# DeltaNet merges in freed buffers, block-wise residual squares, earlier parameters

## The chip, the cores and the metric

The kernel runs on one core of a Trainium2 chip, in one launch. The metric is device time in microseconds (us), from the start of an execution to its end. The engines are TensorE (PE, matmul, with its weight loads as PEld), VectorE (DVE), ScalarE (ACT), GpSimd (POOL) and SyncE (SP, which only issues DMAs here). Each engine runs its own instructions in a fixed order and waits on the others by semaphores. Data sit in SBUF (128 partitions) and in eight PSUM banks, which TensorE writes.

## The reference

A two-layer block for 512 tokens of width 1024: 256 context tokens and 256 latent tokens. Only the latent tokens are returned, so layer 1 needs its context tokens up to the token mixers only. Per layer:

```
mod  = split(silu(c) @ mod_w + mod_b, 6)             # one row for latents, one for context
p    = (rms_norm(h, norm1_g) * (1 + mod[1]) + mod[0]) @ in_w     # (512, 1024) x (1024, 11 K)
y_b  = retention(p), rg_lru(p), gated_deltanet(p), rwkv7(p)       # four branches of width 512
m    = sum_b sigmoid(p_gates_b + gate_b) * (y_b @ branch_w[b])
h    = h + mod[2] * (m @ out_w)
u    = rms_norm(h, norm2_g) * (1 + mod[4]) + mod[3]
h    = h + mod[5] * ((silu(u @ w1) * (u @ w3)) @ w2)
```

The result is `rms_norm(h_latent, final_norm_g)`. The DeltaNet branch has four heads; each works in chunks of tokens, with an inverse of a triangular matrix per chunk and a state that passes from chunk to chunk, in both directions.

## The kernel before

All activations lie transposed: features on partitions, tokens on the free axis. A dense product takes a block of 128 x 128 weights against 512 columns (layer 0) or 256 (layer 1, where only latents are needed). For precision each operand is split into a high and a low part, and a block needs three matmuls: wh·XH, wh·XL and wl·XH (`dense`). Weights are packed on the host in the order of use, in units of 8 blocks (512 KB). `raw` loads a unit on SyncE's queue, `unit` makes wh by a ScalarE cast (L400) and wl by a VectorE subtract (L361). Units are taken in turn from the pools in `wps`: the first one, wp, always, and a second where `more_weights` has opened one.

The work is a list of tasks that `_phases` writes out by hand: `first`, `seq1` (RWKV, retention and RG-LRU with gates ahead), `seq2` (DeltaNet heads `gd` and merges `mg`), `seqo` (output projection `ow`), `seqf` (ffn). `ga(b,d)` computes a gate of branch b ahead of its merge and stores it to HBM (gd), from where `merge` loads it again (t<-gd); `mg(b,d)` does the products of a branch's output with branch_w for two feature blocks, multiplies by the gates and adds into M. `merge_open` loads a branch's output (yt, from HBM's yd) and splits it into YH and YL. A planner then orders the instructions of all engines: among those ready it takes what stands first in the program, so a later task can fill an engine while an earlier one waits. Weight and modulation loads (`early`) go ahead of other work. On the chip each engine keeps that order.

In `layer`, `seq2` runs inside the DeltaNet pool gp with PSUM pools pc2 (two banks, chains) and pd2 (a third dense accumulator `d`). A head `gd` is a serial chain: small matmuls of the inverse into one PSUM tile `mg`, then a loop over four chunks with `Z`, `R` and the state `St` (PSUM tile `ch`), then `headnorm` with transposes (L1260) and `put_y` (L301), which stores the head's output (yd<-to). After seq2 gp is closed, and on its bytes open hh (the residual H, loaded at L1541, and temporaries t2), wo (a second weight pool), mqo (modulation weights) and op (MH, ML, the split of M). A tile of a new pool on old bytes waits for the users of the closed pools there. By the sizes in the code, base pools take about 68 KB of a partition, mp (M, YH, YL, yt, t2) 46 in layer 0 and 27 in layer 1, and gp 92 and 102.

`mod` computes one of the six modulation vectors: weights of 512 KB per k as `mraw` (L592), 4 matmuls per k into the one bank `mg`, a transpose (L603). In layer 0 they stand between other tasks. `squares` squares the eight blocks of H on ScalarE (tile t) and adds them on VectorE; `rms_bcast` sums over partitions by matmuls into `st`, takes the inverse root on VectorE (`sm`), and spreads it by more `st` matmuls; `norm` writes XH and XL. `setup` prepares constants; `load_params` loads a layer's small parameters P, `params_mu` and `params` derive more from them.

Of the kernel before, what the change touches and what calls it, by code (L numbers as in the profile page):

```python
# [11 lines left out]
F32R = mybir.dt.float32r  # L12
# [6 lines left out]
DEPTH = 2  # L19
# [95 lines left out]
def _phases(l):  # L115

    last = l + 1 == DEPTH
    first = _mod(0, 1, 1, 0) + _mod(0, 4, 2) if l == 0 else []
    if last:
        seq1 = [("rws",), ("kvr", 0), ("kvr", 1), ("rw", 0), ("rt", 0), ("lr", 0), *_ga(3, 0, 2), ("kvr", 2), ("rw", 1), ("rt", 1), ("lr", 1), *_ga(3, 2, 4), ("kvr", 3), ("rw", 2), ("rt", 2), ("lr", 2), *_ga(3, 4, 6), ("rw", 3), ("rt", 3), ("lr", 3), *_ga(3, 6, 8)]  # L120
    else:
        seq1 = [("rws",), ("kvr", 0), ("kvr", 1), ("rw", 0), ("rt", 0), ("lr", 0), *_ga(3, 0, 2), ("kvr", 2), ("rw", 1), ("rt", 1), ("lr", 1), *_ga(3, 2, 4), *_ga(0, 0, 2), ("kvr", 3), ("rw", 2), ("rt", 2), ("lr", 2), *_ga(3, 4, 6), *_ga(0, 2, 4), ("rw", 3), ("rt", 3), ("lr", 3), *_ga(3, 6, 8), *_ga(0, 4, 8), *_ga(2, 0, 4)]
    if last:
        seq2 = [*_mg(0, 0, 4), ("gab",), ("gd", 0), ("gd", 1), *_mg(0, 4, 8), *_mg(3, 0, 4), ("gd", 2), *_mg(3, 4, 8), ("gd", 3), *_ga(2, 0, 8), *_mg(1, 0, 8), *_mg(2, 0, 8)]
    else:
        seq2 = [("gab",)] + [("gd", 0)] + _mg(3, 0, 4) + [("gd", 1)] + _mg(3, 4) + [("gd", 2)] + _mg(0, 0, 4) + [("gd", 3)] + _mg(0, 4) + _mg(1) + _mg(2)
    seqo = []
    mo = [] if last else _mod(0, 2, 3, 4)
    for m in range(8):
        seqo += [("ow", m)] + mo[m:m + 1]  # L130
    mf = [] if last else _mod(0, 4, 5) + _mod(1, 4, 0, 1, 2, 3, 4, 5)
    seqf = []
    for f in range(2):
        for j in range(11):
            seqf += [("fi", f, j)]
            if j and len(mf) > 2:
                seqf += mf[:1]
                mf = mf[1:]
        seqf += [("fo", f, m) for m in range(8)]
    seqf += mf  # L140
    return first, seq1, seq2, seqo, seqf


def _ahead(l):
# [1 line left out]
    return {t[1:] for t in _phases(l)[1] + _phases(l)[2] if t[0] == "ga"}  # L146


def _seq(l):
    a, b, c, d, e = _phases(l)  # L150
    return a + b + c + d + e


RWB = 5136
# [52 lines left out]
def _pack(inp):  # L207
# [7 lines left out]
    for l in range(DEPTH):  # L215
# [21 lines left out]
        put(l, "final_g", f["final_norm_g"])  # L237
    mats = {"in_w": f["in_w"], "branch_w": f["branch_w"].reshape(DEPTH, 2048, 1024), "out_w": f["out_w"],
            "ffn_w1": f["ffn_w1"], "ffn_w3": f["ffn_w3"], "ffn_w2": f["ffn_w2"]}
    plan = [(l, b) for l in range(DEPTH) for t in _seq(l) for b in _blocks(t, _ahead(l))]  # L240
    nu = len(plan) // 8
    assert nu * 8 == len(plan)
    W = np.empty((nu, 128, 8, 128), np.float32)
# [24 lines left out]
class Kern:  # L268
# [203 lines left out]
    def setup(self):  # L472
# [25 lines left out]
        for l in range(DEPTH):  # L498
            nc.scalar.dma_start(out=self.modb[:, l], in_=self.ap["P"][l, :, PC["mod_b"]:PC["mod_b"] + 48])
        self.pars = []  # L500

        t = self.sm(16)
        cf = self.cT.rearrange("p k c -> p (k c)")
# [4 lines left out]

        self.sc32 = self.cp.tile([128, 8, 32], F32, name="sc32")
        nc.vector.memset(self.sc32, 0.0)  # L510
        nc.vector.tensor_copy(out=self.sc32[:, :, 0:2], in_=self.sc)

    def load_params(self, l):
# [124 lines left out]
    def rms_bcast(self, c0, S=None):  # L638

        n = 512 - c0  # L640
        nb = n // 128
        S = self.squares(c0) if S is None else S
        ps = self.pst()
        for b in range(nb):
            self.mm(ps[:, b:b + 1], S[:, 128 * b:128 * b + 128], self.c("ones", 0, 1))
        v = self.sm(nb)
        self.ts(v, ps[:, 0:nb], 1.0 / 1024.0, EPS, ALU.mult, ALU.add)
        y = self.rsqrt(v, nb)
        r = self.pst()
        for b in range(nb):  # L650
            self.mm(r[:, 128 * b:128 * b + 128], y[:, b:b + 1].to_broadcast([128, 128]), self.c("ident"))
        return r[:, 0:n]
# [749 lines left out]

    def merge_open(self, b, lat):
        cr = 256 if lat else 0
        self.YH = self.tl(self.mp, [128, 4, 512 - cr], "yh", F32R)
        self.YL = self.tl(self.mp, [128, 4, 512 - cr], "yl", F32R)
        for i in range(4):
            y = self.tl(self.mp, [128, 512 - cr], "yt", bufs=3)
            self.nc.sync.dma_start(out=y, in_=self.yd[b][:, i, cr:512])
            self.split(self.YH[:, i], self.YL[:, i], y)  # L1410
# [4 lines left out]

    def gate_ahead(self, b, d, lat):
        cr = 256 if lat else 0
        g = self.t2(512 - cr)
        self.gate(b, d, cr, g)
        self.nc.sync.dma_start(out=self.gd[b][:, d, cr:512], in_=g)  # L1420

    def merge(self, b, d, lat, first):
        cr = 256 if lat else 0
        G = []
        for dd in (d, d + 1):
            g = self.t2(512 - cr)
            if (b, dd) in self.ahead:
                self.nc.sync.dma_start(out=g, in_=self.gd[b][:, dd, cr:512])
            else:
                self.gate(b, dd, cr, g)  # L1430
            G.append(g)
        for a, dd in enumerate((d, d + 1)):
            ps = self.psd()[:, 0:512 - cr]
            self.dense(ps, lambda k: self.YH[:, k], lambda k: self.YL[:, k], 4)
            m = self.M[:, dd]
            if first:
                self.stt(m, G[a], 1.0, ps, ALU.add, ALU.mult)
            else:
                self.stt(G[a], G[a], 1.0, ps, ALU.add, ALU.mult)
                self.tt(m, m, G[a], ALU.add)  # L1440

    def resid(self, m, ps, q, c0):
        for s in range(c0 // 256, 2):
            a = slice(256 * s - c0, 256 * s - c0 + 256)
            t = slice(256 * s, 256 * s + 256)
            self.stt(self.H[:, m, t], ps[:, a], self.MOD[:, 8 * q + m, s:s + 1], self.H[:, m, t], ALU.mult, ALU.add)

    def layer(self, l):
        nc, tc = self.nc, self.tc
        lat = l == DEPTH - 1  # L1450
        cr = 256 if lat else 0
        first, seq1, seq2, seqo, seqf = _phases(l)
        self.ahead = _ahead(l)
        pool = lambda es, name: es.enter_context(tc.tile_pool(name=f"{name}{l}", bufs=1))

        if l > 0:
            self.__dict__.update(self.pars[l])
        if l == 0:
            with ExitStack() as es:
                es.enter_context(self.mod_stream("mq0", 16))  # L1460
                hp = pool(es, "h0")
                self.tmp = hp, "t2", 10
                self.H = self.tl(hp, [128, 8, 512], "H")
                for k in range(8):
                    nc.scalar.dma_start(out=self.H[:, k], in_=self.ap["xT"][:, k])
                self.load_params(0)
                S = self.squares(0)
                for n, t in enumerate(first):
                    if n == 8:
                        rms = self.rms_bcast(0, S)  # L1470
                    if n == 16:
                        self.norm(0, "norm1_g", 0, 1, rms)
                    self.mod(*t[1:])
                self.params_mu()
            hsrc = self.ap["xT"]
        else:
            self.norm(0, "norm1_g", 0, 1)
# [3 lines left out]
        with ExitStack() as ea:  # L1481
            with ExitStack() as es:
# [13 lines left out]
                for t in seq1:  # L1496
                    if t[0] == "rws":
                        self.rw_shared(lat)
                        if l == 0:
                            self.params(0)  # L1500
                    elif t[0] == "kvr":
                        self.rw_kvr(t[1], lat)
                    elif t[0] == "ga":
# [10 lines left out]
            with ExitStack() as es:  # L1514
# [4 lines left out]
                self.csg = self.tl(self.gp, [128, TW["csg"]], "csg")  # L1519
                nc.scalar.dma_start(out=self.csg, in_=self.ap["csg"])  # L1520
                self.mgb = None
                for t in seq2:
                    if t[0] == "gab":
                        self.gd_ab()
                    elif t[0] == "gd":
                        self.gd_head(t[1], lat)
                    elif t[0] == "ga":
                        self.gate_ahead(t[1], t[2], lat)
                    elif t[0] == "mg":
                        if self.mgb != t[1]:  # L1530
                            self.merge_open(t[1], lat)
                        self.merge(t[1], t[2], lat, self.mgb is None or (self.mgf == t[1]))
                        if self.mgb is None:
                            self.mgf = t[1]
                        self.mgb = t[1]
            self.pds.pop()

            self.hes = ExitStack()
            hp = self.hes.enter_context(tc.tile_pool(name=f"hh{l}", bufs=1, side="right"))
            self.H = self.tl(hp, [128, 8, 512], "H")  # L1540
            nc.sync.dma_start(out=self.H, in_=hsrc)  # L1541
            self.tmp = hp, "t2", 6
            with ExitStack() as es:
                es.enter_context(self.more_weights(f"wo{l}"))
                if not lat:
                    es.enter_context(self.mod_stream(f"mqo{l}", 2))
                op = pool(es, "op")
# [3 lines left out]
                for t in seqo:  # L1551
# [3 lines left out]
                    m = t[1]  # L1555
                    ps = self.psd()[:, 0:512 - cr]
                    self.dense(ps, lambda k: MH[:, k, cr:512], lambda k: ML[:, k, cr:512], 8)
                    self.resid(m, ps, 2, cr)
        self.dbg(f"h1_{l}", self.H)
        self.norm(cr, "norm2_g", 3, 4)  # L1560
        with ExitStack() as es:
# [5 lines left out]
            for t in seqf:  # L1567
# [18 lines left out]
                else:  # L1586
                    ps = self.psd()[:, 0:n]
                    self.dense(ps, lambda k: IH[:, k, cr:512], lambda k: IL[:, k, cr:512], 11)
                    self.resid(t[2], ps, 5, cr)
        self.dbg(f"h2_{l}", self.H)  # L1590

    def final(self):
# [34 lines left out]
```

## Time and profile before

| | |
|---|---|
| median of 3 runs | 2421.22 us (2419.57 to 2421.57) |
| profiled execution | 2415.91 us, span 2414.1 us |
| mean granted TensorE clock | 0.978 of full |
| TensorE busy | 2283.1 us, 95% |
| weight loads (PEld) | 1830.6 us, 76% |
| VectorE busy | 1625.6 us, 67% |
| ScalarE busy | 1033.4 us, 43% |
| GpSimd busy | 56.0 us, 2% |
| moved by DMA | 282.74 MB, 117 GB/s on average |

The span is the time from the first instruction to the last; the execution's own time is a little longer. Matmuls are pipelined, so one matmul's duration is longer than the distance to the next one, and a busy TensorE isn't one at its peak. A row of a timeline ends, where the engine idled before it, with that time and what ended it, in brackets. A window's row gives busy time and, in brackets, the number of instructions for each engine, then the granted clock (1.00 is full), the share of the DMA engines' time and the rate. A few per cent of matmul records may be missing.

### The profile page before, as it was taken

The numbers are of one execution on the slowest core, as the hardware profiler recorded it, in microseconds if no ns is written. First come the engines' busy times: TensorE is split into PE (matmuls) and PEld (weight loads), VectorE is DVE, ScalarE is ACT, GpSimd is POOL, SyncE is SP. The second block draws the span as 40 slices with busy tenths as digits, with TensorE's granted clock in tenths as the row PEclk, the third lists the DMA queues.
The fourth block names the chain that finished last, engine by engine and source line by source line (L and its number), as shares of the span: only waits on it lengthen the run. The fifth ranks groups of instructions, "written<-read, shape, count | busy, mean of one in ns | idle before, by whom it ended". The sixth has DMA issues, their size and how long they took to land. (4 is left out here: it accounts for less than half of the span.)

```text
span 2414.1 us, 48292 instructions
## 1 busy us (share of the span) xinstructions
PE 2283.1 (95%) x19400; PEld 1830.6 (76%) x19400; DVE 1625.6 (67%) x4644; ACT 1033.4 (43%) x2014; POOL 56.0 (2%) x154
## 2 busy tenths in 40 slices
PE   5999999999999999989999988999999999988998
PEld 3777777677788877667787867777777888877998
DVE  5686959695498955363333336988888689866565
ACT  3454545444444433232222224655565454544443
POOL 0000000000000000000000000000000000000000
PEclk9999999999999999989999999999999899998999
DMA  7312131214423234736634322122222342454663
GB/s 301 96 45 83 49 94 40 87 45 130 127 88 102 83 131 168 255 120 231 214 96 157 96 89 85 56 79 61 75 67 63 114 132 86 135 193 132 185 185 112
DMA packets 91376, 282.74 MB, mean 117 GB/s; under 512 B 10512, under 2 KB 21008, under 8 KB 90768
## 3 DMA queue, kind: packets, MB, share of 16 engines
q1 hardware_dynamic: 86256, 271.62, 35.2%
q10 hardware_dynamic: 4896, 8.03, 1.1%
q8 instruction: 153, 2.51, 0.4%
q14 instruction: 71, 0.58, 0.1%
HBM read 262.83 MB, written 16.78 MB: 116 GB/s over the span
## 5 line engine op out<-in xcount | busy, mean ns | idle before, releaser
L343 PE MATMUL d<-XH,wh 128*128 128x512 f32 (+1 forms) x2112 | 765.5, 364 | 17.1 <-ACT XH L340 10.9
L343 PE MATMUL d<-XH,wl 128*128 128x512 f32 (+1 forms) x2112 | 761.9, 361 | 1.0 <-DVE wl L361 1.0
L343 PE MATMUL d<-XL,wh 128*128 128x512 f32 (+1 forms) x2112 | 760.9, 360 | 1.8 <-DVE XL L368 1.8
L400 ACT CAST wh<-raw 128x1024 fp32r<-128x1024 f32 x356 | 372.8, 1048 | 746.2 <-PE d L343 437.1
L361 DVE TENSOR_TENSOR wl<-raw,wh 128x1024 fp32r<-128x1024 f32 x356 | 435.1, 1223 | 355.1 <-ACT wh L400 350.3
L343 PEld LDWEIGHTS d<-XH,wh 128*128 128x128 f32 x2112 | 400.8, 190 | 90.7 <-ACT XH L340 13.4
L343 PEld LDWEIGHTS d<-XH,wl 128*128 128x128 f32 x2112 | 400.7, 190 | 64.7 <-issue 6.7
L343 PEld LDWEIGHTS d<-XL,wh 128*128 128x128 f32 x2112 | 401.3, 190 | 62.0 <-DVE XL L368 3.2
L368 DVE SCALAR_TENSOR_TENSOR t<-t,d 128x512 f32<-128x512 f32 (+1 forms) x136 | 74.5, 551 | 74.0 <-PE d L343 67.5
L343 PE MATMUL d<-ih,wh 128*128 128x512 f32 (+1 forms) x352 | 118.6, 337 | 0.0
L343 PE MATMUL d<-ih,wl 128*128 128x512 f32 (+1 forms) x352 | 118.3, 336 | 0.0
L343 PE MATMUL d<-il,wh 128*128 128x512 f32 (+1 forms) x352 | 118.3, 336 | 0.0
L343 PE MATMUL d<-yh,wh 128*128 128x512 f32 (+1 forms) x256 | 88.4, 353 | 7.7 <-ACT yh L439 5.0
L343 PE MATMUL d<-yl,wh 128*128 128x512 f32 (+1 forms) x256 | 91.0, 356 | 1.8 <-DVE yl L361 1.8
L343 PE MATMUL d<-yh,wl 128*128 128x512 f32 (+1 forms) x256 | 88.8, 348 | 0.2 <-DVE wl L361 0.2
L368 DVE SCALAR_TENSOR_TENSOR H<-d,MOD,H 128x256 f32<-128x256 f32 x72 | 32.8, 480 | 78.9 <-PE d L343 78.8
L343 PE MATMUL mg<-mraw,sc 128*32 128x256 f32 x768 | 55.7, 420 | 21.9 <-DMA mraw<-in_WM_dram 16.0
L343 PEld LDWEIGHTS d<-ih,wh 128*128 128x128 f32 x352 | 66.8, 190 | 7.5 <-issue 0.4
L343 PEld LDWEIGHTS d<-il,wh 128*128 128x128 f32 x352 | 66.8, 190 | 6.9
L343 PEld LDWEIGHTS d<-ih,wl 128*128 128x128 f32 x352 | 66.8, 190 | 6.9
L343 PEld LDWEIGHTS mg<-mraw,sc 128*32 128x32 f32 x768 | 23.0, 116 | 50.3 <-DMA mraw<-in_WM_dram 22.4
L343 PEld LDWEIGHTS d<-yh,wh 128*128 128x128 f32 x256 | 48.9, 194 | 14.2 <-ACT yh L439 6.5
(358 smaller groups left out, 3549.2 us busy)
## 6 DMA issues: line engine op xcount, KB each, us to landing
raw<-in_W_dram SPq DMA_DIRECT2D x356, 512.0 KB, 3.6
mraw<-in_WM_dram SPq DMA_DIRECT2D x96, 512.0 KB, 6.7
gd<-tm SPq DMA_DIRECT2D x20, 256.0 KB, 3.1
t<-gd SPq DMA_DIRECT2D x20, 256.0 KB, 3.5
yt<-yd SPq DMA_DIRECT2D x16, 256.0 KB, 4.0
H<-in_xT_dram ACTq DMA_DIRECT2D x8, 256.0 KB, 6.8
lrw<-in_LW_dram ACTq DMA_DIRECT2D x8, 256.0 KB, 2.7
yd<-tr SPq DMA_DIRECT2D x8, 256.0 KB, 3.6
```

The source lines that it names most:

```text
L343: i = self.nc.tensor.matmul(out=out, lhsT=lhsT, rhs=rhs, start=start, stop=stop, skip_group_check=chk).ins
L361: self.nc.vector.tensor_tensor(out=out, in0=a, in1=b, op=op)
L368: self.nc.vector.scalar_tensor_tensor(out=out, in0=a, scalar=s, in1=b, op0=op0, op1=op1)
L400: self.nc.scalar.copy(wh, r3)
```

## The change

The last merges leave `seq2` for a list `tail`, which runs after gp, pc2 and pd2 are closed; H's pool, wo, two new PSUM banks (pd3, pd4), and a second pool mb for YH and YL are open for it. In layer 1 the gates of branch 2 are kept in SBUF (gk) instead of going through HBM. In layer 0 six modulation tasks stand between the tail's merges; the later lists of modulation shrink by them. The residual's squares are taken per block inside `resid`, and block 7's square goes to the matmuls as a second term. Layer 0's parameters are loaded and derived in `setup`.

```diff
 def _phases(l):
-    first = _mod(0, 1, 1, 0) + _mod(0, 4, 2) if l == 0 else []
+    first = _mod(0, 1, 1, 0) if l == 0 else []
...
-        seq2 = [*_mg(0, 0, 4), ("gab",), ("gd", 0), ("gd", 1), *_mg(0, 4, 8), *_mg(3, 0, 4), ("gd", 2), *_mg(3, 4, 8), ("gd", 3), *_ga(2, 0, 8), *_mg(1, 0, 8), *_mg(2, 0, 8)]
+        seq2 = [*_mg(0, 0, 4), ("gab",), ("gd", 0), ("gd", 1), *_mg(0, 4, 8), *_mg(3, 0, 4), ("gd", 2), *_mg(3, 4, 8), ("gd", 3)]
+        tail = [*_ga(2, 0, 8), *_mg(1, 0, 8), *_mg(2, 0, 8)]
     else:
-        seq2 = [("gab",)] + [("gd", 0)] + _mg(3, 0, 4) + [("gd", 1)] + _mg(3, 4) + [("gd", 2)] + _mg(0, 0, 4) + [("gd", 3)] + _mg(0, 4) + _mg(1) + _mg(2)
+        seq2 = [("gab",)] + [("gd", 0)] + _mg(3, 0, 4) + [("gd", 1)] + _mg(3, 4) + [("gd", 2)] + _mg(0, 0, 4) + [("gd", 3)]
+        tail = _mg(0, 4)
+        ms = _mod(0, 4, 2, 3, 4)
+        for t in _mg(1) + _mg(2):
+            tail += [t] + ms[:1]
+            ms = ms[1:]
-    mo = [] if last else _mod(0, 2, 3, 4)
+    mo = [] if last else _mod(0, 2, 5)
...
-    mf = [] if last else _mod(0, 4, 5) + _mod(1, 4, 0, 1, 2, 3, 4, 5)
+    mf = [] if last else _mod(1, 4, 0, 1, 2, 3, 4, 5)
...
-            if j and len(mf) > 2:
+            if j % 2 or j == 10:
...
-    seqf += mf
 def setup(self):
...
+        self.load_params(0)
...
+        self.params_mu()
+        self.params(0)
         nc.vector.tensor_copy(out=self.sc32[:, :, 0:2], in_=self.sc)
 def rms_bcast(self, c0, S=None):
-        S = self.squares(c0) if S is None else S
+        S = self.S if S is None else [S]
         for b in range(nb):
-            self.mm(ps[:, b:b + 1], S[:, 128 * b:128 * b + 128], self.c("ones", 0, 1))
+            for a, x in enumerate(S):
+                self.mm(ps[:, b:b + 1], x[:, 128 * b:128 * b + 128], self.c("ones", 0, 1), start=a == 0, stop=a + 1 == len(S))
 def merge_open(self, b, lat):
-        self.YH = self.tl(self.mp, [128, 4, 512 - cr], "yh", F32R)
-        self.YL = self.tl(self.mp, [128, 4, 512 - cr], "yl", F32R)
+        self.mo += 1
+        mp = self.mps_[self.mo % len(self.mps_)]
+        self.YH = self.tl(mp, [128, 4, 512 - cr], "yh", F32R)
+        self.YL = self.tl(mp, [128, 4, 512 - cr], "yl", F32R)
 def gate_ahead(self, b, d, lat):
+        if self.gk is not None:
+            g = self.kept[b, d] = self.tl(self.gk, [128, 512 - cr], "gk", bufs=8)
+            self.gate(b, d, cr, g)
+            return
 def resid(self, m, ps, q, c0, last):
...
+        if last:
+            sq = self.t2(512 - c0)
+            self.act(sq, self.H[:, m, c0:512], AF.Square)
+            if m == 0:
+                self.S = [sq]
+            elif m < 7:
+                self.tt(self.S[0], self.S[0], sq, ALU.add)
+            else:
+                self.S.append(sq)
 def layer(self, l):
...
             hp = self.hes.enter_context(tc.tile_pool(name=f"hh{l}", bufs=1, side="right"))
             self.H = self.tl(hp, [128, 8, 512], "H")
-            nc.sync.dma_start(out=self.H, in_=hsrc)
             self.tmp = hp, "t2", 6
             with ExitStack() as es:
                 es.enter_context(self.more_weights(f"wo{l}"))
+                self.pds += [es.enter_context(tc.tile_pool(name=f"pd{j}{l}", bufs=1, space=PSUM)) for j in (3, 4)]
+                with ExitStack() as eb:
+                    if lat:
+                        self.gk = pool(eb, "gk")
+                    else:
+                        eb.enter_context(self.mod_stream(f"mqb{l}", 6))
+                    mb = pool(eb, "mb")
+                    self.mps_ = [mb, self.mp] if self.mo % 2 else [self.mp, mb]
+                    for n, t in enumerate(tail):
+                        if n == 2:
+                            nc.sync.dma_start(out=self.H, in_=hsrc)
+                        if t[0] == "mod":
+                            self.mod(*t[1:])
+                        else:
+                            run2(t)
```

## Rows read from the trace of the kernel before

**Rows 1.** Windows around places where TensorE idles: busy us (instructions) by engine, granted clock, DMA share.

```profile
0.00:44.80 44.80, 18.85 (x146) 7.81 (x146) 21.38 (x125) 11.46 (x22) 0.20 (x4) 1.00 0.98 376
1015.00:1037.60 22.60, 10.05 (x97) 6.18 (x96) 14.18 (x54) 7.01 (x15) 0.00 (x0) 0.72 0.83 303
1431.50:1453.10 21.60, 7.50 (x80) 5.43 (x79) 10.21 (x31) 6.63 (x17) 0.57 (x2) 0.65 0.35 125
2149.00:2189.00 40.00, 28.66 (x193) 26.70 (x193) 26.13 (x46) 17.59 (x28) 0.00 (x0) 0.87 0.75 260
```

**Rows 2.** Windows over the last two DeltaNet heads of each layer, all engines.

```profile
804.60:889.90 85.30, 84.47 (x825) 67.51 (x825) 63.01 (x193) 34.33 (x91) 2.92 (x9) 1.00 0.25 73
2055.50:2148.10 92.60, 88.28 (x1112) 82.12 (x1110) 71.31 (x237) 44.10 (x100) 3.44 (x7) 1.00 0.45 135
```

**Rows 3.** The same windows, instructions of the accumulator `d` alone.

```profile
804.60:889.90 85.30, 60.98 (x227) 39.91 (x227) 6.16 (x9) 4.01 (x6) 1.00 0.25 73
2055.50:2148.10 92.60, 68.96 (x480) 59.37 (x478) 4.52 (x10) 7.81 (x17) 1.00 0.45 135
```

**Rows 4.** Timeline of SyncE's queue, end of layer 0's heads: start, us, operation, count.

```profile
888.77 0.33 SPq L301 DMA_DIRECT2D yd<-to  x1
889.90 1.84 SPq L391 DMA_DIRECT2D raw<-in_W_dram  x2
```

**Rows 5.** Timeline of SyncE's queue, end of layer 1's heads.

```profile
2146.46 0.33 SPq L301 DMA_DIRECT2D yd<-to  x1
...
2148.09 3.05 SPq L391 DMA_DIRECT2D raw<-in_W_dram  x4
```

**Rows 6.** Windows of steady dense work, accumulator `d`, layer 0 and layer 1.

```profile
920.00:960.00 40.00, 39.41 (x170) 31.31 (x169) 3.93 (x6) 2.73 (x4) 1.00 0.35 114
2220.00:2260.00 40.00, 40.00 (x341) 39.06 (x341) 5.85 (x14) 2.61 (x7) 1.00 0.58 177
```

**Rows 7.** Costs of one weight unit: parts 5 and 6 of the page.

```profile
L400 ACT CAST wh<-raw 128x1024 fp32r<-128x1024 f32 x356 | 372.8, 1048 | 746.2 <-PE d L343 437.1
L361 DVE TENSOR_TENSOR wl<-raw,wh 128x1024 fp32r<-128x1024 f32 x356 | 435.1, 1223 | 355.1 <-ACT wh L400 350.3
...
raw<-in_W_dram SPq DMA_DIRECT2D x356, 512.0 KB, 3.6
```

**Rows 8.** Timeline of ScalarE and VectorE in a state step of layer 1's last head.

```profile
2122.54 0.39 ACT L340 ACTIVATE Z<-ch 128x256 f32<-128x256 f32 x1 [2.36 <-PE ch L343]
...
2124.92 1.23 DVE L361 TENSOR_TENSOR wl<-raw,wh 128x1024 fp32r<-128x1024 f32 x1
...
2127.51 0.39 ACT L340 ACTIVATE Z<-ch 128x256 f32<-128x256 f32 x1 [2.62 <-PE ch L343]
```

**Rows 9.** Timeline of TensorE, first chain matmuls of the heads gd 2.

```profile
803.17 0.62 PE L343 MATMUL mg<-q,q 32*32 32x32 f32 x50
...
2068.78 0.70 PE L343 MATMUL mg<-q,q 32*32 32x32 f32 x60
```

**Rows 10.** Window of layer 1's last RWKV pair, all engines.

```profile
1841.00:1893.00 52.00, 42.45 (x576) 34.49 (x576) 33.81 (x112) 24.19 (x47) 2.21 (x2) 0.80 0.26 77
```

**Rows 11.** Timeline of TensorE around layer 0's second and layer 1's first norm.

```profile
1019.84 4.42 PE L343 MATMUL mg<-mraw,sc 128*32 128x256 f32 x64 [0.55 <-DVE t L603]
1029.62 1.87 PE L343 MATMUL st<-cstt,t 128*128 128x1 f32 x8 [5.36 <-DVE t L361]
...
1431.39 3.66 PE L343 MATMUL mg<-mraw,sc 128*32 128x256 f32 x64
1445.24 1.87 PE L343 MATMUL st<-cstt,t 128*128 128x1 f32 x8 [10.19 <-DVE t L361]
```

**Rows 12.** Timeline of VectorE in the start, with the wait ahead of it.

```profile
23.84 0.25 DVE L365 TENSOR_SCALAR dmu<-P 128x15 f32<-128x15 f32 x2 [6.05 <-DMA P<-in_P_dram]
```

**Rows 13.** Windows with the sums' matmuls (tile `st`) at either clock.

```profile
28.00:38.00 10.00, 3.94 (x16) 3.56 (x16) 0.16 (x1) 0.00 (x0) 1.00 1.03 406
1028.00:1042.00 14.00, 3.94 (x16) 3.56 (x16) 3.81 (x10) 0.00 (x0) 0.51 0.62 247
```

More of the change, by code (lines that the diff above doesn't have):

```diff
@@ L139, in _phases, with _kept @@
         seqf += [("fo", f, m) for m in range(8)]
-    seqf += mf
-    return first, seq1, seq2, seqo, seqf
+    assert not mf
+    return first, seq1, seq2, tail, seqo, seqf
 def _ahead(l):
     return {t[1:] for t in _phases(l)[1] + _phases(l)[2] if t[0] == "ga"}
+def _kept(l):
+    return {t[1:] for t in _phases(l)[3] if t[0] == "ga"}
 def _seq(l):
-    a, b, c, d, e = _phases(l)
-    return a + b + c + d + e
+    return sum(_phases(l), [])
 RWB = 5136
@@ L239, in _pack @@
             "ffn_w1": f["ffn_w1"], "ffn_w3": f["ffn_w3"], "ffn_w2": f["ffn_w2"]}
-    plan = [(l, b) for l in range(DEPTH) for t in _seq(l) for b in _blocks(t, _ahead(l))]
+    plan = [(l, b) for l in range(DEPTH) for t in _seq(l) for b in _blocks(t, _ahead(l) | _kept(l))]
     nu = len(plan) // 8
@@ L1425, in merge @@
         for dd in (d, d + 1):
+            if (b, dd) in self.kept:
+                G.append(self.kept.pop((b, dd)))
+                continue
             g = self.t2(512 - cr)
@@ L1440, in merge, with merge_task, resid @@
                 self.tt(m, m, G[a], ALU.add)
-    def resid(self, m, ps, q, c0):
+    def merge_task(self, t, lat):
+        if t[0] == "ga":
+            self.gate_ahead(t[1], t[2], lat)
+            return
+        if self.mgb != t[1]:
+            self.merge_open(t[1], lat)
+        self.merge(t[1], t[2], lat, self.mgb is None or (self.mgf == t[1]))
+        if self.mgb is None:
+            self.mgf = t[1]
+        self.mgb = t[1]
+    def resid(self, m, ps, q, c0, last):
         for s in range(c0 // 256, 2):
@@ L1451, in layer @@
         cr = 256 if lat else 0
-        first, seq1, seq2, seqo, seqf = _phases(l)
+        first, seq1, seq2, tail, seqo, seqf = _phases(l)
         self.ahead = _ahead(l)
+        self.kept, self.gk, self.mo = {}, None, 0
         pool = lambda es, name: es.enter_context(tc.tile_pool(name=f"{name}{l}", bufs=1))
@@ L1465, in layer @@
                     nc.scalar.dma_start(out=self.H[:, k], in_=self.ap["xT"][:, k])
-                self.load_params(0)
                 S = self.squares(0)
@@ L1470, in layer @@
                         rms = self.rms_bcast(0, S)
-                    if n == 16:
-                        self.norm(0, "norm1_g", 0, 1, rms)
                     self.mod(*t[1:])
-                self.params_mu()
+                self.norm(0, "norm1_g", 0, 1, rms)
             hsrc = self.ap["xT"]
@@ L1498, in layer @@
                         self.rw_shared(lat)
-                        if l == 0:
-                            self.params(0)
                     elif t[0] == "kvr":
@@ L1521, in layer @@
                 self.mgb = None
+                self.mps_ = [self.mp]
+                run2 = lambda t: self.merge_task(t, lat)
                 for t in seq2:
@@ L1526, in layer @@
                         self.gd_head(t[1], lat)
[L1527 to L1535, printed above, removed]
+                    else:
+                        run2(t)
             self.pds.pop()
@@ L1544, in layer @@
                 es.enter_context(self.more_weights(f"wo{l}"))
+                self.pds += [es.enter_context(tc.tile_pool(name=f"pd{j}{l}", bufs=1, space=PSUM)) for j in (3, 4)]
[11 more added lines that the diff above has]
+                            self.mod(*t[1:])
+                        else:
+                            run2(t)
                 if not lat:
@@ L1557, in layer @@
                     self.dense(ps, lambda k: MH[:, k, cr:512], lambda k: ML[:, k, cr:512], 8)
-                    self.resid(m, ps, 2, cr)
+                    self.resid(m, ps, 2, cr, True)
+                self.pds = self.pds[:2]
         self.dbg(f"h1_{l}", self.H)
@@ L1588, in layer @@
                     self.dense(ps, lambda k: IH[:, k, cr:512], lambda k: IL[:, k, cr:512], 11)
-                    self.resid(t[2], ps, 5, cr)
+                    self.resid(t[2], ps, 5, cr, t[1] == 1)
         self.dbg(f"h2_{l}", self.H)
```

## The prediction

> **What bounds the kernel now.** I read the busy part of the page first: TensorE works 95% of the span, so what is left to win is its idle time, about 131 us by the table of the profile (2414.1 − 2283.1), and the question for each edit is whether it fills TensorE's idle time or makes new. The table of windows says where much of it lies [rows 1]: 26 us before the first dense product at 44.8, 12.6 and 14.1 us around two norms (1015 to 1037.6, 1431.5 to 1453.1), 11.3 us at the end of layer 1's merges. The same view over the last two DeltaNet heads of each layer [rows 2] shows the opposite: 84.47 of 85.30 us busy in layer 0, 88.28 of 92.60 in layer 1, at full clock. These heads are serial chains of small matmuls and short VectorE and ScalarE steps, so something else fills TensorE there. Restricted to the dense accumulators `d`, the view counts it [rows 3]: 227 matmuls after gd 3's input projection in layer 0, 480 in layer 1. By program order these are mg(0,4..8), mg(1) and the start of ga/mg work that stands behind gd 3, which is the work that the change calls tail.
>
> **Part 1: the tail is put behind the DeltaNet pool.** The deciding fact is what a new pool on old bytes waits for. By the code's sizes all the tail's pools (hh, wo, mqb or gk, mb) land on bytes of gp, and PSUM pd3 and pd4 on banks of pc2 and pd2. Today hh, wo and mqo do that, and SyncE's timeline [rows 4] shows when they open: gd 3's last store yd<-to is issued at 888.77, and 1.1 us later, at 889.90, two weight loads go out at once. Layer 1 is the same [rows 5]: store 2146.46, then four weight loads at once from 2148.09. Different tiles are released at one moment, after the last head's last reader; nothing of them goes earlier, though a head uses many of gp's tiles only in its first half. So I take it that no tail task with a new tile runs before the last head has stored its y. One weight unit (8 blocks, 24 matmuls) can run early out of the first pool; then SyncE's queue, which is in order, stands at the next unit, and everything behind it (merge inputs, H, modulation) stands too.
>
> Price. Behind the release fall 227 − 24 = 203 matmuls in layer 0 and 480 − 24 = 456 in layer 1. The pace of dense stretches is 39.41/170 = 0.232 us for 512 columns and 40.00/341 = 0.117 us for 256 [rows 6]: 47.1 and 53.5 us. The refill costs a load, a cast and a subtract before the first product of the new units: 3.6 + 1.05 + 1.22 = 5.9 us [rows 7], per layer.
>
> Against it, the heads get faster when the fill is gone. In layer 1 a step of the state loop takes 2127.51 − 2122.54 = 4.97 us from one Z to the next, and one weight subtract of 1.23 us, which is tail work, stands on VectorE in it [rows 8], with the state's next operation behind it: a quarter. Taken over both heads, from their first chain matmul at 803.17 and 2068.78 [rows 9] to the release at 889.90 and 2148.09, 86.7 and 79.3 us, a quarter is 21 and 20 us; I use 20 for each. Bounds: 0, if the chain's own latencies fill the time; and 40%, 33 us, if besides the subtract some 0.8 us goes of the time in which Z waits on TensorE (2.36 and 2.62 us [rows 8]), where its matmuls stand behind dense ones. I stay at the quarter since it is the part that a row shows.
>
> Layer 0: 47.1 + 5.9 − 20 = +33. Layer 1: 53.5 + 5.9 − 20 = +39. Both restarts come after a thinly used TensorE. The nearest row for that is the last RWKV pair of layer 1, where fill ran out [rows 10]: 42.45 of 52 us busy, mean granted clock 0.80. I put +3 for dense products begun at the lower level. Part 1 is +75; its bounds are +49 (40%) and +115 (nothing saved).
>
> Merges also get a second pair of YH/YL buffers (mb) and two more PSUM banks. That takes away the gaps at branch changes; in layer 1 the gates no longer go out to HBM and back behind the 2 MB load of H. The window 2149 to 2189 has 11.3 us without TensorE and a clock of 0.87 [rows 1]. MH/ML's splits still wait for the last merge, since their pool lies on gk and mb, about 4 to 5 us: I count −7, and −3 for the clock (0.13 × 40 us is 10 us at half speed if one level is 1.2 and the other 2.4 GHz, of which half goes). Bounds −3 to −13.
>
> **Part 2: squares block by block.** Today all eight squares and seven adds run after the last residual. The sums' matmuls start at 1029.62 (5.36 us waiting for t) and, in layer 1, 1445.24 (10.19) [rows 11], while the dense work before them ended at about 1015.0 and 1431.5. After the change seven blocks are done inside the products; what is left is the last block's update and square, about 2 us, so they start at about 1017.0 and 1433.5: 12.6 and 11.7 us earlier. Twice as many of these matmuls (one row's group of 8 took 1.87 us) gives back 1.87 each. Gain 10.7 + 9.8 = −20.5. Cover: 8 squares on ScalarE, and the adds on VectorE, beside the products of `ow` and `fo`; over the span these engines are 43% and 67% busy. Without that cover the old waits of 5.36 and 10.19 us are what it costs. The layer-1 norm and the final one have half the columns and short gaps; −0.5 against +0.6, nothing.
>
> **Part 3: modulation moved.** The two gaps hold 64 modulation matmuls each today, 4.42 and 3.66 us [rows 11], which hid there for nothing; now they stand in dense stretches: with a short group before the first, +9. Their loads are in SyncE's queue ahead of time (8 buffers in the ffn). If they are late in the tail, their 512 KB loads at the release compete with weights, yt, gates and H for the same DMA engines; I leave that out, its bound is +10. Clock around the two norms (0.72 and 0.65 [rows 1]) improves as the gaps halve: −3.
>
> **Part 4: parameters first.** VectorE waits 6.05 us for P until 23.84 [rows 12], in the midst of the first norm, because the derived parameters stand ahead of the squares' adds in its order, and modulation's transpose comes behind their logarithms. With P early this goes: −4.5. Bounds −1 and −6: until the first dense product the DMA engines are 0.98 busy [rows 1], so it soon ends at the loads. The q 2 product's 2 tasks leave the start too; they are counted in this.
>
> **Sum.** +75 − 10 − 20.5 + 9 − 3 − 4.5 = +46. The profiled execution took 2415.9 us (span 2414.1), so 2462; the median of the runs is 5.3 above the profiled one, so 2467.
>
> **Rivals.**
> A, the heads nearly free themselves: each layer's two heads lose 33 us instead of 20. For it: chain matmuls queue behind dense ones. Against: the waits in [rows 8] are mostly latencies of four dependent steps. 2467 − 26 = 2441.
> B, the chains don't get shorter, because thin work lets TensorE's clock fall, and what the fill cost is lost to it: 2467 + 40 = 2507. For it: the clock of 0.80 in [rows 10]. Against: the group of 16 sum matmuls takes 3.94 us in a window at 1.00 and in one at 0.51 alike [rows 13]; small matmuls here are all latency. The Trainium skill (TensorE: Matmul & The Clock Gate, Back-to-back issue gap) gives a gap between matmuls that scales with columns at either level, nearly doubling at the low one. By that rule the heads' 128-column products would slow with the clock and B would be the outcome; the row of 16 does not bear it out, so B keeps a small chance.
> C, the other side: buffers come free tile by tile, or the bytes in question are released before gd 3. Then tail work fills the heads as today, Part 1's +75 is gone, and the rest stays: −29, 2392. It decides from where the release costs less than about 14 us a layer, that is at about 851 in layer 0 and 2104 in layer 1 instead of my 870 and 2128. For it: gp holds many tiles that only early parts of a head use. Against: the loads at one moment in [rows 4, 5], when these pools wait today.
>
> **How the numbers follow.** Forecast 0.70, A 0.12, B 0.08, C 0.10. The predicted time is the forecast's, 2467. Its terms' bounds give 2432 (A with the large ends of the gains) to 2500 (a third of the way into B's loss, or late loads in both layers). Outside that lie C, the end of B and a little of A: 2 in 10. A measurement tells this kernel from no change at about 0.2%, 5 us. Faster is C less the part of it that ends near zero, 0.10; same 0.02; slower 0.88.
>
> **What would show it.** Right: in the changed kernel's SyncE timeline, no loads into the second weight pool, no yt and no H before the last yd<-to of a layer, which comes at about 870 (shifted by the start's gain) and 2128 plus the first layer's loss; dense matmuls missing beneath gd 2's tail and gd 3, with a granted clock below 1 there; a Z-to-Z step near 3.7 us; the sums' matmuls within 3 us after the last `ow` and `fo`; P used without a wait. Wrong: `d` matmuls of mg(1) between gd 3's first and last chain matmul (C), or an unchanged step (B). If the first dense product doesn't come before 43, Part 4 is nothing. If modulation's loads delay weights after a release, the refill is over 10 us.

## The result

The changed kernel takes 2500.24 us (median of 4 runs, 2496.36 to 2504.21) against 2420.39 us for the kernel before beside it: ratio 1.0342, interval 1.0322 to 1.0361, so 3.4% slower. The forecast was 2467 and slower; the direction held, the loss was 80 us where 46 were forecast, and the time lies just above the upper end of the range, 2500. The page of the changed kernel (busy time, then three rows of 40 slices: granted clock, DMA share, GB/s; its span is 2494.7 us):

```profile
PE 2310.7 (93%) x19424; PEld 1853.5 (74%) x19424; DVE 1626.6 (65%) x4640; ACT 1035.0 (41%) x2014; POOL 54.9 (2%) x154
...
PEclk8999999999999779999999999999998999599999
DMA  6212131215332075553535333122222342064653
GB/s 233 91 40 84 44 105 40 81 40 177 105 99 65 5 261 168 205 172 123 188 99 181 123 103 91 58 80 67 68 65 73 117 134 63 3 222 145 186 185 113
```

TensorE's busy time rose by 28 us and the span by 80.6; the clock fell from 0.978 to 0.956 on average. Slices 14 and 35 hold the end of the two layers' heads: hardly any DMA (5 and 3 GB/s) and a clock of 7 and 5 tenths. Windows over those stretches and over the gaps:

```profile
799.50:878.10 78.60, 47.96 (x622) 39.32 (x622) 42.24 (x165) 20.84 (x74) 2.90 (x9) 0.78 0.06 19
891.80:914.20 22.40, 6.73 (x64) 2.74 (x64) 1.91 (x2) 0.81 (x1) 0.00 (x0) 0.71 0.92 317
1086.20:1095.10 8.90, 7.30 (x89) 4.84 (x89) 5.94 (x27) 4.05 (x8) 0.00 (x0) 1.00 0.89 301
1487.80:1497.40 9.60, 3.89 (x23) 3.43 (x23) 4.69 (x22) 3.01 (x10) 0.56 (x2) 0.71 0.75 280
2095.90:2189.90 94.00, 59.80 (x681) 49.23 (x679) 47.70 (x203) 21.28 (x67) 2.55 (x7) 0.60 0.07 22
```

Against [rows 2] TensorE is busy for 47.96 of 78.60 us in layer 0 and 59.80 of 94.00 in layer 1, at a clock of 0.78 and 0.60. The norms' gaps of [rows 1], 22.6 and 21.6 us, are 8.9 and 9.6. The second row is new: 22.4 us with no dense product at all. The accumulators `d` alone, in the same stretches of the heads, where [rows 3] had 227 and 480 matmuls:

```profile
799.50:878.10 78.60, 6.83 (x24) 4.13 (x24) 0.67 (x1) 0.60 (x1) 0.78 0.06 19
2095.90:2189.90 94.00, 7.08 (x49) 6.76 (x47) 1.89 (x3) 0.40 (x1) 0.60 0.07 22
```

In layer 0 24 are left; in layer 1 49: 24 right behind gd 3's projection, 24 at the head's end, and the projection's last. The release is where the forecast put it, behind the last store. SyncE's queue at the end of layer 0's heads (compare [rows 4]) and of layer 1's ([rows 5]):

```profile
877.03 0.33 SPq L311 DMA_DIRECT2D yd<-to  x1
879.50 0.33 SPq L401 DMA_DIRECT2D raw<-in_W_dram  x1
879.88 0.43 SPq L605 DMA_DIRECT2D mraw<-in_WM_dram  x1
...
888.37 1.38 SPq L605 DMA_DIRECT2D mraw<-in_WM_dram  x3
...
894.74 10.79 SPq L605 DMA_DIRECT2D mraw<-in_WM_dram  x8
905.58 2.72 SPq L1451 DMA_DIRECT2D t<-gd  x4
908.34 0.61 SPq L1589 DMA_DIRECT2D H<-in_xT_dram  x1
```

```profile
2188.82 0.41 SPq L311 DMA_DIRECT2D yd<-to  x1
2192.79 0.81 SPq L401 DMA_DIRECT2D raw<-in_W_dram  x2
2193.64 0.43 SPq L1589 DMA_DIRECT2D H<-hd  x1
```

The span's difference by stages, from the dense products' first start and last end in both traces:

| stage | before | after | difference | forecast |
|---|---|---|---|---|
| start to gd 3's projection, layer 0 | 804.8 | 799.5 | −5.3 | −4.5 |
| to the last `ow`, layer 0 | 210.2 | 286.7 | +76.5 | +33, and half of +3 |
| norm 2, ffn, norm 1 of layer 1 | 438.1 | 411.2 | −26.9 | −20.5 − 3 + 9 |
| mixers of layer 1 to gd 3's projection | 602.4 | 598.5 | −3.9 | 0 |
| to the last `ow`, layer 1 | 146.6 | 187.2 | +40.6 | +39 − 10, and half of +3 |
| ffn and end | 212.0 | 211.6 | −0.4 | 0 |

### The profile page after: what moved, and what is told of

Same layout as the page of the kernel before. It is cut to its first block, busy times and chain, and to the rows that moved or that the text cites. A ratio compares the mean times of both kernels' runs of the same rounds, so it can differ in the third digit from the quotient of the medians.

```text
span 2494.7 us, 48292 instructions
## 1 busy us (share of the span) xinstructions
PE 2310.7 (93%) x19424; PEld 1853.5 (74%) x19424; DVE 1626.6 (65%) x4640; ACT 1035.0 (41%) x2014; POOL 54.9 (2%) x154
## 5 line engine op out<-in xcount | busy, mean ns | idle before, releaser
L378 DVE SCALAR_TENSOR_TENSOR t<-t,d 128x512 f32<-128x512 f32 (+1 forms) x128 | 71.2, 558 | 92.9 <-PE d L353 68.8
L353 PE MATMUL d<-yh,wh 128*128 128x512 f32 (+1 forms) x256 | 89.1, 351 | 12.5 <-ACT wh L410 8.0
```

What stands on the lines that cost most here:

```text
L353: i = self.nc.tensor.matmul(out=out, lhsT=lhsT, rhs=rhs, start=start, stop=stop, skip_group_check=chk).ins
L378: self.nc.vector.scalar_tensor_tensor(out=out, in0=a, scalar=s, in1=b, op0=op0, op1=op1)
```

## Experiments

In all of them the ratio is to runs of the kernel before on the same chip. Diffs are shortened; `...` marks what is left out.

**e1: the tail back under the heads.** Both `tail` lists return to `seq2`, the tail's pools go, the modulation lists are those of before; the block-wise squares and the early parameters stay.

```diff
-        seq2 = [..., ("gd", 3)]
-        tail = [*_ga(2, 0, 8), *_mg(1, 0, 8), *_mg(2, 0, 8)]
+        seq2 = [..., ("gd", 3), *_ga(2, 0, 8), *_mg(1, 0, 8), *_mg(2, 0, 8)]
+        tail = []
...
-        seq2 = ... + [("gd", 3)]
-        tail = _mg(0, 4)
...
+        seq2 = ... + [("gd", 3)] + _mg(0, 4) + _mg(1) + _mg(2)
+        tail = []
...
```

> The tail stands inside the DeltaNet pool again (both layers), modulation lists as before the change; what stays of the change is the squares by block and the parameters first. Theory (the whole loss comes from the tail behind the heads, the rest gains): 2393 to 2410, with squares' matmuls within 8 us of the last out projection. Rival (the squares or the parameters cost something too): 2420 or more.

Measured 2387.53 us, ratio 0.9881 (0.9862 to 0.9900), a little under the theory's range; the sums' matmuls start within 2 us of the last out projection's end (1012.93 after 1011.2). So what stays is worth 1.2%, and the tail with all that opens for it, modulation included, costs some 111 us (1.0342 − 0.9881 = 0.0461 of 2418). The norms' gaps of e1, from the last `ow` or `fo` to the next dense product:

```profile
1011.20:1023.70 12.50, 9.72 (x83) 5.79 (x81) 8.96 (x37) 4.54 (x10) 0.00 (x0) 0.73 0.49 160
1416.40:1427.90 11.50, 7.56 (x89) 5.57 (x89) 5.20 (x22) 3.07 (x10) 0.56 (x2) 0.76 0.64 235
```

12.5 and 11.5 us, where [rows 1] had 22.6 and 21.6.

**e2: modulation as before, the tail stays behind the heads.** `first`, `mo` and `mf` as in the kernel before, no modulation in `tail`, no mqb.

```diff
-            tail += [t] + ms[:1]
-            ms = ms[1:]
+            tail += [t]
...
```

> The change with the modulation lists of before, so no modulation loads between the layer-0 tail's merges. Theory (in layer 0 the burst of modulation loads ahead of the merge inputs in SyncE's queue makes the hole between 892 and 914): 2476 to 2488, the first mg(1) product within 12 us of the last head's store instead of 37. Rival (the refill by weights, gates and H makes the hole by itself): 2495 to 2505.

Measured 2487.68, ratio 1.0299 (1.0283 to 1.0316). The first product of mg(1) starts 16 us after the last store (899.7, store 883.57) instead of 37, not within 12. From gd 3's projection to the last `ow` layer 0 takes 255.8 us instead of 286.7; of these 31 us, 6.6 are paid before it (2.1 of them by the first dense product, 44.3 instead of 42.2, where q 2's tasks are back in the start; the rest is not traced) and 13.7 after it (norms and ffn, 424.9 instead of 411.2). Modulation in the tail explains 31 of layer 0's +76.5; the rest, 45.6, is the tail itself. Against e1, the tail without its modulation still costs 1.0299 − 0.9881 = 0.0418 of 2418, 101 us.

**e3: extra matmuls under the heads gd 2 and gd 3.** Each group stands behind a group of the chain on TensorE: 2 after each group of the state loop, 2 to 4 in the inverse, 16 before the norm. The result is not used.

```diff
+    def fill(self, n):
...
+        for _ in range(n):
+            i = self.nc.tensor.matmul(out=self.fb, lhsT=self.XH[:, 0, 0:128], rhs=self.XH[:, 0, 0:512], start=True, stop=True).ins
+            self.tc.add_manual_dep(i, self.lastmm.name, ...)
...
+            self.fill(2)
...
```

> The change with extra 512-column matmuls into a spare bank, each group pinned behind a matmul group of the chains of gd 2 and gd 3 in both layers; their result is not used. Theory (the heads did not get shorter because TensorE's clock fell to half under them): clock 1.00 through the heads, each of the four heads 5 to 9 us shorter, 2465 to 2482. Rival (the heads' length is latency of dependent steps, the clock costs them nothing): heads within 2 us of those of the change, 2495 to 2512.

Measured 2507.76, ratio 1.0380 (1.0351 to 1.0409): by the time, neither. The extra accumulator took a third `d` bank away from gd 3's projection, which ended at 830.1 instead of 799.5. The heads themselves speak for the theory: from first matmul to store gd 3 took 35.5 us in layer 0 and 33.6 in layer 1, where the changed kernel has 40.4 and 39.6; gd 2 of layer 1 took 36.9 instead of 41.3, and gd 2 of layer 0, which the changed kernel runs at full clock but for its last 7 us, 38.1 instead of 38.6. Since the late projection confounds the time, e5 repeats this under one head.

**e5: the same under gd 3 alone.** `fb` is taken from the third bank after the last projection (diff against e3).

```diff
-        if h == 2:
-            self.fp2 = self.pds.pop()
...
+        if h == 3:
+            self.fb = self.tl(self.pds.pop(), [128, 512], "d")
```

> As e3, but the extra matmuls (unused results) stand behind the chain of gd 3 alone, so that no projection of a later head is moved. In e3's trace the heads that had run at the low clock were 4.4 to 5.9 us shorter. Theory (that was the clock): gd 3 takes 34 to 36 us in both layers instead of 40.4 and 39.6 from its first matmul to its store, the time 8 to 12 us under that of the change: 2484 to 2492. Rival (the extra matmuls change nothing in the time, because what follows a release waits for DMA and not for the head): 2496 to 2504.

Measured 2494.82, ratio 1.0313 (1.0279 to 1.0347). Windows of gd 3, first chain matmul to store, layer 0 and layer 1: first e5, then the changed kernel, then the kernel before.

```profile
842.29:877.96 35.67, 33.24 (x380) 24.80 (x380) 11.22 (x38) 8.04 (x28) 0.78 (x2) 0.95 0.02 9
2150.18:2184.05 33.87, 31.70 (x366) 23.03 (x367) 10.13 (x38) 6.51 (x21) 0.78 (x2) 0.91 0.02 5
```

```profile
836.60:877.03 40.43, 25.18 (x324) 20.73 (x324) 12.28 (x39) 8.31 (x28) 0.78 (x2) 0.67 0.07 21
2149.26:2188.82 39.56, 27.26 (x322) 22.87 (x322) 11.26 (x39) 7.33 (x22) 0.78 (x2) 0.55 0.01 5
```

```profile
851.39:888.77 37.38, 37.16 (x412) 29.32 (x413) 19.73 (x49) 13.76 (x35) 0.78 (x2) 1.00 0.20 59
2109.13:2146.46 37.33, 35.49 (x488) 33.02 (x487) 21.82 (x54) 16.04 (x34) 0.79 (x2) 1.00 0.39 118
```

35.67 and 33.87 us at a clock of 0.95 and 0.91, as the theory said, against 40.43 and 39.56 at 0.67 and 0.55. The time came out between both sides and its interval overlaps that of the changed kernel. Of the 4.8 and 5.7 us that the heads became shorter, 2.2 and 2.5 are left at the last `ow` of their layers. In layer 0 part of it is gone before the release: the store comes 74.7 us after gd 3's projection instead of 77.5, since gd 2, which has no extra matmuls, took 40.58 us instead of 38.64, for a reason that stays open. The kernel before, with VectorE doing twice the work beside it, needed 37.38 and 37.33.

**e7: the tail's modulation loads without priority.**

```diff
-    def mod(self, l, q, k0, n):
+    def mod(self, l, q, k0, n, early=True):
...
-            with self.early():
+            with self.early() if early else ExitStack():
...
-                            self.mod(*t[1:])
+                            self.mod(*t[1:], early=False)
```

> The change with the tail's modulation loads issued in program order instead of ahead of other work, so that the merge's branch outputs and H stand before them in SyncE's queue. Theory (the hole of 22 us after mg(0,6) in layer 0 is the queue: 12 loads of 512 KB ahead of the branch output): hole under 8 us without modulation, 2476 to 2490. Rival (all these bytes must pass before dense work can go on steadily, the order only moves the hole): 2494 to 2504.

Measured 2483.37, ratio 1.0264 (1.0226 to 1.0302), below the changed kernel's interval. SyncE's queue and TensorE where the hole was:

```profile
882.56 0.33 SPq L311 DMA_DIRECT2D yd<-to  x1
885.03 0.80 SPq L401 DMA_DIRECT2D raw<-in_W_dram  x2
885.88 1.97 SPq L1451 DMA_DIRECT2D t<-gd  x4
...
893.56 0.43 SPq L1589 DMA_DIRECT2D H<-in_xT_dram  x1
...
901.22 0.42 SPq L605 DMA_DIRECT2D mraw<-in_WM_dram  x1
```

```profile
897.36 0.39 PE L353 MATMUL d<-yh,wl 128*128 128x512 f32 x1
897.59 0.39 PE L353 MATMUL d<-XH,wh 128*128 128x512 f32 x1
```

The gates (t<-gd) and H now come ahead of the modulation (mraw), and the first mg(1) product follows mg(0,6) at matmul pace. The hole was the order of the queue. What I had named in it, the branch output, was wrong: the gates are what was late. In the changed kernel, TensorE and the one long wait of VectorE over that stretch:

```profile
884.17 0.79 PE L353 MATMUL d<-yh,wh 128*128 128x512 f32 x1 [7.95 <-ACT wh L410]
...
891.37 0.39 PE L353 MATMUL d<-yh,wl 128*128 128x512 f32 x1
894.01 3.25 PE L353 MATMUL mg<-mraw,sc 128*32 128x256 f32 x32 [2.26 <-DMA mraw<-in_WM_dram]
901.52 3.48 PE L353 MATMUL mg<-mraw,sc 128*32 128x256 f32 x32 [4.26 <-DMA mraw<-in_WM_dram]
914.23 0.80 PE L353 MATMUL d<-XH,wh 128*128 128x512 f32 x1 [9.23 <-DVE t L378]
```

```profile
DVE t L378 <- DMA t<-gd: 19.6, 1, 19.6
```

mg(0,6)'s products end at 891.8, VectorE multiplies them by gates whose loads were issued at 905.58, behind 14 of modulation, and until then the accumulators are not free: 9.23 us of waiting for t, and 2.26 and 4.26 for modulation weights before it.

**e4: only mg(2) in the tail.**

```diff
-        seq2 = [..., ("gd", 3)]
-        tail = [*_ga(2, 0, 8), *_mg(1, 0, 8), *_mg(2, 0, 8)]
+        seq2 = [..., ("gd", 3), *_ga(2, 0, 8), *_mg(1, 0, 8)]
+        tail = _mg(2, 0, 8)
...
-        seq2 = ... + [("gd", 3)]
-        tail = _mg(0, 4)
...
+        seq2 = ... + [("gd", 3)] + _mg(0, 4) + _mg(1)
+        tail = _mg(2)
...
```

> Only mg(2), the one merge that needs the last head, stays in the tail; everything else of the tail is back under the heads, modulation lists as before. Theory (the loss is the work taken from under the heads, not the new buffers): 2385 to 2408, at most 6 us off the version with the whole tail back. Rival (opening the tail's pools at the release costs by itself): 2412 or more.

Measured 2398.39, ratio 0.9928 (0.9912 to 0.9944): in the theory's range of times, but 11 us behind e1 instead of at most 6. The stretch of the tail is not where it loses: layer 0's first `ow` product starts at 960.3 (e1: 959.9). What it loses, 9 us in the traces, appears in the second norm of layer 0 (16.6 us instead of 12.5), in the ffn (396.5 instead of 392.7) and in the `ow` products (52.4 instead of 51.3); in the gap modulation waits 1.56 us for its weights. Why these stretches grew is not shown, so the new pools may have a part in it. In the merges themselves they neither cost nor gain anything that shows.

**e8: the squares by block alone, in the kernel before.**

```diff
+        if last:
+            sq = self.t2(512 - c0)
+            self.act(sq, self.H[:, m, c0:512], AF.Square)
...
```

> The kernel before with the squares by block alone. Theory (the two norms' gaps carry nearly all that e1 gained, 10 us each): 2392 to 2400, e1 less than 8 us below it. Rival (the parameters first are worth as much, the earlier start moves more than the first norm): 2402 to 2412.

Measured 2392.87, ratio 0.9894 (0.9862 to 0.9926): 25.6 us, nearly all of e1's gain, and 21.8 of it lie in the two gaps (10.9 and 11.5 us instead of 22.6 and 21.6). e1's 0.9881 lies inside its interval: the early parameters are not told from nothing, 3 us by the medians and 1.5 at the first dense product (43.8 in e1, 45.2 here).

**e9: e1 with modulation moved out of the norms' gaps.** The diff is against e1.

```diff
-        seqo += [("ow", m)] + mo[m:m + 1]
+        seqo += mo[m:m + 1] + [("ow", m)]
...
-            if j and len(mf) > 2:
+            if j:
...
-    seqf += mf
```

> e1 (tail under the heads) with the modulation tasks of layer 0 put ahead of the products they follow, and none left behind the last ffn product, so that no modulation matmul stands in the two norms' gaps. In e1's trace 64 of them (3.7 us) stand before the sums' matmuls of layer 1's first norm and some 7 us of them in layer 0's second. Theory: 2379 to 2386. Rival (they only move to another busy stretch): 2386 to 2390.

Measured 2390.05, ratio 0.9887 (0.9854 to 0.9919), no different from e1. The time is the rival's, but the edit cleared one gap only:

```profile
1015.70:1029.10 13.40, 10.00 (x105) 5.69 (x103) 8.40 (x36) 4.17 (x9) 0.00 (x0) 0.87 0.81 259
1423.90:1434.50 10.60, 3.96 (x26) 3.49 (x24) 4.83 (x22) 3.06 (x10) 0.57 (x2) 0.67 0.69 255
```

The second gap is 10.6 us instead of 11.5, with TensorE 3.96 us busy in it instead of 7.56 and no modulation matmul left. The first grew from 12.5 to 13.4 and holds 80 of them, where e1's holds 58. So what modulation costs in the first gap is not tested. e1 remains the best version measured, 1.2% under the kernel before.

## Why the prediction was right in direction and wrong in size

**What held.** Nothing of a new pool goes before the closed pool's last reader, so 203 products in layer 0 and about 430 in layer 1 (456 were forecast) fell behind the release ([rows 3] against the windows above). e1 shows that the tail turns a gain into a loss, and e2 that it does so without its modulation too. C (tiles freed one by one) is refuted by the same rows. The sums' matmuls follow the last `ow` and `fo` within 2 us, as forecast. The squares were forecast at −20.5 with −3 for the clock; e8 shows −25.6. The start was forecast at −4.5 and the stage gave −5.3, but only 2.6 of it stand at the first dense product (42.2 instead of 44.8), and what part the parameters have in them is not shown.

**The step that failed** is "Taken over both heads, ... a quarter is 21 and 20 us; I use 20 for each." From gd 3's projection to the last store the changed kernel needs 77.5 us in layer 0 (before: 84.0) and 92.9 in layer 1 (before: 91.0): 6.4 us less and 2.0 more. Of the 20 and 20, 35.6 us are missing. That this is nearly the 34.6 between forecast and measured span is chance: the second miss below adds to the loss, and what was too gloomy takes about as much away. Two things were wrong in the step.

First, a step of the state loop was taken for the whole head. In gd 2 of layer 0, at full clock up to 829.6, the changed kernel's inverse takes 13.02 us as before, the loop 15.57 instead of 17.53, the norm's part up to the transposes 8.81 instead of 10.99. Under the inverse nearly the same work ran in both kernels, one unit's subtract and the products of mg(0,4) that the first pool let through (16 and 12), so little could be taken away there. In the loop a step went from 4.88 (823.43 to 828.31) to 4.30 us, 12%, not a quarter; that most of the subtract's time was time in which R had to wait anyway is my reading. In layer 1, where the forecast took its row, a step at full clock can be read in e5: 4.47 us (2168.01 to 2172.48) against 4.97, 10%, with the extra matmuls beside it, where 3.7 was forecast. And 5.3 of layer 0's 6.4 us are no shorter head at all: between gd 2's store and gd 3's first matmul the kernel before lets 5.43 us pass (845.96 to 851.39) and the changed one 0.12 (836.48 to 836.60). The Z rows of gd 2 in layer 0, in the kernel before and in the changed one, then of the changed one in layer 1, and last of gd 3 of layer 1 in e5:

```profile
823.43 0.39 ACT L340 ACTIVATE Z<-ch 128x256 f32<-128x256 f32 x1
...
828.31 0.39 ACT L340 ACTIVATE Z<-ch 128x256 f32<-128x256 f32 x1
```

```profile
816.72 0.38 ACT L350 ACTIVATE Z<-ch 128x256 f32<-128x256 f32 x1
...
821.02 0.38 ACT L350 ACTIVATE Z<-ch 128x256 f32<-128x256 f32 x1
```

```profile
2128.35 0.38 ACT L350 ACTIVATE Z<-ch 128x256 f32<-128x256 f32 x1 [4.58 <-PE ch L353]
...
2134.32 0.38 ACT L350 ACTIVATE Z<-ch 128x256 f32<-128x256 f32 x1
```

```profile
2168.01 0.38 ACT L351 ACTIVATE Z<-ch 128x256 f32<-128x256 f32 x1 [3.09 <-PE ch L354]
...
2172.48 0.38 ACT L351 ACTIVATE Z<-ch 128x256 f32<-128x256 f32 x1
```

Second, that step is 5.97 us long in the changed kernel's layer 1. The clock was at half there for 68 us on end (2116.4 to 2184.7), with little but the chain's short matmuls left on TensorE; e5, which puts matmuls between them, got 0.91. The chain's own matmuls at either level in the changed kernel (the clock fell at 829.6): the first group of gd 2 and of gd 3 in layer 0, and a group with Z in layer 0 and in layer 1:

```profile
797.84 0.75 PE L353 MATMUL mg<-q,q 32*32 32x32 f32 x64
...
817.16 0.71 PE L353 MATMUL ch<-Z,kd 128*128 128x128 f32 x4 [0.77 <-ACT Z L350]
...
836.60 1.08 PE L353 MATMUL mg<-q,q 32*32 32x32 f32 x64 [0.94 <-DVE to L378]
...
2134.75 1.23 PE L353 MATMUL ch<-Z,kd 128*128 128x128 f32 x4 [0.56 <-ACT Z L350]
```

The 64 matmuls of 32 columns take 0.75 us at the full clock and 1.08 at half, the 4 of 128 columns 0.71 and 1.23. I had put B at 0.08 because 16 sum matmuls seemed to take 3.94 us at either level [rows 13]. That reading was wrong. The trace of the kernel before has no record of the clock before 38.4 us, and for such a stretch the view prints 1.00. The changed kernel's trace has one from 13.8 us on, and the same 16 matmuls in its start take the same 3.94 us at a clock of 0.51; by these times the start of the kernel before was at the low level too. At full clock, in its second norm of layer 0, 14 of one column take 1.72 us and 8 of 128 columns 1.16 (tile `st`):

```profile
28.00:38.00 10.00, 3.94 (x16) 3.56 (x16) 0.16 (x1) 0.00 (x0) 0.51 1.01 399
1088.00:1089.80 1.80, 1.72 (x14) 1.64 (x14) 0.00 (x0) 0.00 (x0) 1.00 0.95 348
1092.20:1093.50 1.30, 1.16 (x8) 0.97 (x8) 0.00 (x0) 0.00 (x0) 1.00 1.04 413
```

At the low level 8 of either kind take 1.87 [rows 11] and 2.08 us. So there was no row against B: the small matmuls slow down with the clock. The Trainium skill (TensorE: Matmul & The Clock Gate, Back-to-back issue gap) lets the gap between matmuls grow with the columns at either level and nearly double at the low one. The 128-column rows agree with that, with 1.16 and 2.08 us. B's mechanism is what happened in layer 1, and in gd 3 of layer 0. e5 prices it at 4.8 and 5.7 us for its two heads, and e3 gives 4.4 for gd 2 of layer 1. By my estimate from these the clock is some 15 of the 35.6 us, and the quarter itself the other 20.

**The second miss** is "I leave that out, its bound is +10" for modulation loads at the release. In layer 0 they cost 31 us up to the last `ow` (e2), 20 of which e2 pays elsewhere, and 19 us in the whole time by their place in the queue alone (e7: 0.0342 − 0.0264 = 0.0078 of 2418). What was worst placed was not weights or H but the small gate loads, which hold accumulators. I counted the bytes on the DMA engines and not the order of the queue that issues them.

**Where it was too gloomy.** Layer 1 with its missing 22 us of shorter heads would have come to +52; it came to +40.6. After the release its merges have almost no gap: from 2193.3 to 2283.1 TensorE stands still for about 2 us. Gates kept in SBUF and the second YH/YL pair would explain that, but no run takes them apart from the rest. The stage with the norms gave 12.4 us more than forecast: the two gaps shrank by 25.7 us, and the +9 for modulation doesn't show between them (the ffn takes 392.7 us instead of 393.9). These two, and 3.9 us in layer 1's mixers which were not forecast and whose cause stays open, are what kept the loss from being larger still.

Not settled: how long a head would be with nothing at all beside it at full clock in layer 1; the extra matmuls of e5 stand in its way too. And why e5's shorter last heads did not show fully in layer 1's time; 6.8 us at the store (86.1 instead of 92.9 after gd 3's projection) are 2.5 at the last `ow`.

## What to carry to other kernels

Before moving work behind a pool that must close, count what that work fills: here TensorE was 99 and 95% busy under serial chains only because the merges ran there, and some 50 us of products a layer came out from under them. Don't expect a chain to get shorter by what is taken from beside it; look at every phase of it, and at the clock that the thin rest will be granted. When several loads were released at once, the queue's order decided: put the load that frees an accumulator first, whatever its size. And before a row with a clock of 1.00 carries a step, see that the trace has a record of the clock there.

## What the runs showed that I had not expected

A serial chain of short matmuls that keeps TensorE busy for 27.26 of 39.56 us (2149.26 to 2188.82) was granted the lower clock nearly throughout, as it was for 68 us on end over two heads, while the same chain with 512-column matmuls between its groups had 0.91. And the doubled sum matmuls of the norms, priced at +1.87, cost next to nothing, for a reason that was not in the forecast: in e1's second norm of layer 0 the 16 take 0.28 and 1.72 us at full clock, where 8 took 1.87 at half [rows 11]. The clock, not their number, was what they had cost.
